# A third combined block a layer in a four-branch decoder trunk: 256 features of two branches side by side

## Chip, cores and metric

The kernel runs on one core of a Trainium2 chip. The metric is the device time of one execution in microseconds (us), the median of several runs; a profiled execution gives the trace.

## What is computed

Two layers on x of 512 tokens by 1024 features, in float32. In each, h = rmsnorm(x) is projected to the inputs of four token mixers, which give four branch outputs o of 256 features each, to four gates and to 4 x 1024 merge logits. What the change touches is the end of a layer:

```python
for i, o in enumerate((o_nsa, o_pool, o_conv, o_fox)):
    branch = (o * jax.nn.silu(gates[:, :, i])) @ w_branch[i]
    term = jax.nn.sigmoid(merge[:, :, i]) * branch
    acc = term if acc is None else acc + term
return x + acc @ w_out
```

`merge` is h times 1024 x 4096 weights, `w_branch[i]` is 256 x 1024 and `w_out` 1024 x 1024.

## The kernel before, in words

**Products.** TensorE (PE) takes a rounded 32-bit format, so every operand is split into a high and a low part, and a product is three matmuls (high-high, low-high, high-low). `split` makes the parts: ACT copies to the high part (L72), VectorE (DVE) subtracts for the low one (L73).

**Weights.** `Stream` (L93) brings the 80 weight tiles of a layer (128 x 1024, 512 KB) from `w_all`, in a fixed order, on the queue of SyncE (SP), into three buffers "wr". A tile's buffer is free again when DVE has made its low part. From `more` (L137) on, the merge weights may also go into four other places: the buffer of the rope tables and the three thirds of "V", the attention values, which come free with the last product of probabilities and V (L698). Two weights that are to be added are either added by DVE (L928) or by an accumulating load on the POOL queue (L125).

**A layer.** Dense projections (`dense`, L288: 24 matmuls of 128 x 512 at L303, evacuated by DVE at L324), then 12 attention units (scores L652, softmax on DVE and ACT L655 to L667, transposes L676, products with V L698) with `filler` dense projections between them, among them the first merge logits (`LOGITS`; `AHEAD` = 2 tiles are taken ahead). Then the end of the layer, in three parts:
- the dense part: features 0 to 511 of the merge, 16 logit tiles in feature-major form. For each m of four (L1224), `branches(m)` (L821, 24 matmuls at L832; evacuated at L837 and L841) and four `dense` of `LOGITS`. Between the matmuls of these goes `combine_h` (L850), 20 side steps and four more: it loads x tiles again ("ptc", two buffers, SP, L860), scales them on ACT (L867), sums them on DVE (L877 to L885) and splits the sums, four each for the products P7, P6, P3 and P5.
- `merge` (L955): features 512 to 1023 in two combined blocks, each of two branches, with tokens and inputs in halves. Seven products P1, P2, P7, P6, P5, P3, P4 (L988; 168 matmuls of 512 columns) give what eight would (192). P7 and P6 need the sums of x. Then 48 branch matmuls (L1026), tanh on ACT, sums on DVE. `prepare` (L909) and `merge_ahead` add and split the weights one or two products ahead.
- transposes to feature-major form, the output projection, and the residual; in layer 1 in two halves of the tokens, followed by the last norm. `add_square` and `sum_squares` (L230 to L260) make the norm's sum of squares.

**What sets the order.** The program is recorded in the order of the code and then reordered: a scheduler puts each engine's instructions into one fixed sequence, and each engine (and each engine's DMA queue) takes its own strictly in that order, waiting where a semaphore asks for it.

Of the kernel before, what the change touches and what calls it, by code (L numbers as in the profile page):

```python
# [20 lines left out]
NTILE = 80  # L21
MERGE0 = 52
FILL = 7
ACT_NORM = ()
HID = (9, 11, 13, 15)
GATES = [(0, 0), (2, 0), (0, 1), (2, 1), (1, 0), (3, 0), (1, 1), (3, 1)]
LOGITS = [(m, i) for m in range(4) for i in range(4)]
AHEAD = 2
# [16 lines left out]
def trunk_kernel(ctx: ExitStack, tc: tile.TileContext, xT, w_all, par_all, const, gains, rope, outT):  # L45
# [11 lines left out]
    def sb(shape, tag, bufs, dt=F32):  # L57
        return work.tile(shape, dt, tag=tag, name=tag, bufs=bufs)
# [34 lines left out]
    class Stream:  # L93
        def __init__(self):
            self.order, self.added = [], set()
            for l in range(L):
                self.order += [(l, i) for i in range(MERGE0)]
                for b in range(2):
# [12 lines left out]
            self.raw, self.parts = {}, {}  # L111
# [42 lines left out]
        def load(self, slot="wr"):  # L154
            i = self.loaded
            self.loaded += 1
            c = self.cols(i)
            self.slots.pop(next(n for n, x in enumerate(self.slots) if x is slot))
            if slot == "wr":
                t = sb([128, 1024], "wr", 3)  # L160
            elif slot == "rope":
                t = sb([128, 2, T], "rope", 1).rearrange("p a b -> p (a b)")
            else:
                t = slot
            l, j = self.order[i]
            if i == 0:
                for n in range(2):
                    nc.scalar.dma_start(t[:, n * 512:n * 512 + 512], w_all[l, j, :, n * 512:n * 512 + 512])
            else:
                nc.sync.dma_start(t[:, :c], w_all[l, j, :, :c])  # L170
            self.raw[i] = t, slot
# [65 lines left out]

    def add_square(src, m, bias=0.0, sq=None):
        n = src.shape[-1]
        sq = (temp() if sq is None else sq)[:, :n]  # L240
        ACT.activation(sq, src, AF.Square, bias=bias)
        if m in (0, 7):
            state["sq"] = sq
        else:
# [4 lines left out]
            else:  # L249
                DVE.tensor_tensor(state["sq"], state["sq"], sq, ALU.add)  # L250
            if m == 6:
                sum_squares(n, True, False)

    def stats(n=T, keep=False):
        sum_squares(n, False, True)
        p = state["ssq"]
# [652 lines left out]
    def prepare():  # L909
# [10 lines left out]

        for blk in range(2):
            t2 = [None, None]
# [32 lines left out]
    def merge(l, side, ah, al, lead):  # L955
# [6 lines left out]
        def tanh(dst, src, tok):  # L962
            ACT.activation(dst, src, AF.Tanh, scale=rth[:, tok:tok + 1])

        acc = [None] * 4
        for bp in range(2):
            X = Y = W = None
            sig = {}
            s1, u2, u4 = [None] * 2, [None] * 2, [None] * 2
            for name in PRODUCTS:  # L970
                if name == "P1":
# [8 lines left out]
                for h in range(2):  # L980
                    wh, wl = take_ready()
                    for tt in range(2):
# [8 lines left out]
                        if h == 0 and tt == 0:  # L991
                            merge_ahead(2)
                    merge_ahead(2)
                for tt in range(2):
                    if name in ("P1", "P6", "P5"):
                        t = sb([128, T], "p", 5) if name == "P5" and bp == 0 else temp()
                        ACT.activation(t, X[tt], AF.Copy)
                        {"P1": s1, "P6": u2, "P5": u4}[name][tt] = t
# [8 lines left out]
                    elif name == "P3":  # L1007
                        t = temp() if bp else sb([128, T], "p", 5)
                        tanh(t, X[tt], 4 + tt)
# [7 lines left out]
            for j, toks in ((1, (2, 3, 0, 1)), (0, (0, 1, 2, 3))):  # L1017
                wh, wl = take_ready()
                for tok in toks:
                    p = psum(*next(banks))  # L1020
                    n = 0
                    for kt in range(2):
                        yh, yl = state["y"][2 * bp + j, kt]
                        c, d = slice(tok * 128, tok * 128 + 128), slice(kt * 512, kt * 512 + 512)
                        for x, w in ((yh, wh), (yl, wh), (yh, wl)):
                            PE.matmul(p, x[:, c], w[:, d], start=(n == 0), stop=(n == 5))  # L1026
                            n += 1
                    sg = sig[j, tok]
# [15 lines left out]
        for f in range(4):  # L1044
            pt = psum("pt", 2)
            for tok in range(4):
                PE.transpose(pt[:, tok * 128:tok * 128 + 128], acc[tok][:, f * 128:f * 128 + 128], ident)
            h, lo = sb([128, T], "y", 16, F32R), sb([128, T], "y", 16, F32R)
            split(h, lo, pt, scale=0.5)
            ah.append(h)  # L1050
            al.append(lo)


    nc.gpsimd.dma_start(ng, gains)
    xr = []
# [16 lines left out]
    idle = psum("s", 2)  # L1072
    for n in range(16):
        PE.matmul(idle[:, 128:T], tri_ones[:, 128:256], tri_ones[:, 128:T], start=n == 0, stop=n == 15)

# [18 lines left out]
    for l in range(L):  # L1094
# [140 lines left out]
        if l + 1 < L:  # L1235
# [13 lines left out]
        else:  # L1249
            xn = []  # L1250

            def ev_last(m, c):
                def g(acc):
# [3 lines left out]
                    DVE.tensor_tensor(x, acc[:, :c.stop - c.start], x, ALU.add)  # L1257
                    add_square(x, m)
                    if m == 1:
# [29 lines left out]
    for half in range(2):  # L1289
# [3 lines left out]
        drain()  # L1293
        _, rb = stats(T // 2, keep=True)
        x = xn[KT - 1][:, c]
# [56 lines left out]
def _layout(np, a):  # L1352
# [8 lines left out]
    for l in range(L):  # L1361
# [22 lines left out]
        logit = [feat(run(3472 + 1024 * i + 128 * m)) for m, i in LOGITS]  # L1384
        for m in range(4):
            tiles += logit[4 * m + (AHEAD if m else 0):4 * m + 4 + AHEAD]
            tiles.append(a["w_branch"][l].reshape(8, 128, 1024)[:, :, m * 128:m * 128 + 128]
                         .transpose(1, 0, 2).reshape(128, 1024))
        for bp in range(2):
            for kh in range(2):  # L1390
# [44 lines left out]
```

## Time and profile before

| | before |
|---|---|
| median of 3 runs | 954.16 us (953.74 to 955.42) |
| profiled execution | 953.55 us |
| span of its trace | 951.0 us |
| PE busy | 936.2 us, 98% |
| DVE busy | 714.0 us, 75% |
| ACT busy | 520.0 us, 55% |
| DMA | 124.73 MB, mean 131 GB/s |

The span is the time between the trace's first and last event; the execution's own time has 2.6 us around it. Busy time is the sum of what an engine worked; the chain is the work and the waits that lead to the end, followed backwards. A group's mean is of its instructions' own durations, and PE's matmuls overlap, so a stream's pace is taken from the chain, not from the mean.

### The profile page before, as it was taken

To read this page: it belongs to the slowest core of one execution; us is meant where nothing else is said; L and a number is where in the kernel's file an instruction comes from. 1 tells how busy PE (TensorE), PEld (TensorE's weight loads), DVE (VectorE), ACT (ScalarE), POOL (GpSimd) and SP (SyncE) were. 2 spreads that over 40 slices of the span, in tenths; PEclk is the share of its full clock that TensorE was granted. 3 is DMA by queue.
4 is the path that set the end of the run, shared out by engine and by line. 5 is a ranking of instruction groups with operands and counts; after the bars stand their busy time and mean duration, and the time that the engine had idled before them with its cause. 6 is when DMAs were issued, how large, how long until landed. Compare 5 with 4: busy or idle time off the path is not lost.

```text
span 951.0 us, 12852 instructions
## 1 busy us (share of the span) xinstructions
PE 936.2 (98%) x4696; PEld 795.4 (84%) x4696; DVE 714.0 (75%) x1392; ACT 520.0 (55%) x906; POOL 31.1 (3%) x45
## 2 busy tenths in 40 slices
PE   9999999999999999999999999999999999999996
PEld 7988888888878888887889888888888788888796
DVE  6694689986787977776668548999677878686765
ACT  7295475575545554544426636656665455546273
POOL 0000000000000000000100000000000000010002
PEclk9999999999999999999999999999999999999998
DMA  7253222222236667643515421221322557686353
GB/s 268 80 175 113 74 83 68 78 89 89 67 122 173 171 207 213 177 155 134 189 63 170 135 89 67 89 67 45 111 67 79 177 159 201 200 210 194 112 168 121
DMA packets 39614, 124.73 MB, mean 131 GB/s; under 512 B 4464, under 2 KB 6528, under 8 KB 39552
## 3 DMA queue, kind: packets, MB, share of 16 engines
q1 hardware_dynamic: 35712, 112.38, 36.0%
q0 software_dynamic: 2976, 10.50, 5.5%
q10 hardware_dynamic: 864, 1.05, 0.3%
q8 instruction: 36, 0.59, 0.3%
q14 instruction: 26, 0.21, 0.1%
HBM read 119.72 MB, written 4.19 MB: 130 GB/s over the span
## 4 chain that ended last, share of the span: by engine, by line
PE 95%; DVE 2%; ACT 1%; DMA 1%; issue 1%; POOL 0%; DVEq 0%; SPq 0%; ACTq 0%; POOLq 0%
PE ps_d L303 56%; PE ps_d L988 9%; PE ps_s L988 5%; PE ps_o L698 3%; PE ps_pt L676 3%; PE ps_pt L988 2%; PE ps_pt L1026 2%; PE ps_s L554 2%; PE ps_pt L554 2%; PE ps_s L832 2%; PE ps_s L653 2%; PE ps_s L652 1%; PE ps_pt L832 1%; PE ps_o L1026 1%; PE ps_d L1026 1%; PE ps_o L415 1%
## 5 line engine op out<-in xcount | busy, mean ns | idle before, releaser
L303 PE MATMUL ps_d<-xh,wh 128*128 128x512 f32 x632 | 248.9, 394 | 1.9 <-ACT wh L72 1.9
L303 PE MATMUL ps_d<-xl,wh 128*128 128x512 f32 x632 | 248.6, 394 | 0.5 <-DVE xl L76 0.5
L72 ACT ACTIVATE wh<-wr 128x1024 fp32r<-128x1024 f32 (+2 forms) x134 | 139.0, 1038 | 153.9 <-PE ps_d L303 70.1
L73 DVE TENSOR_TENSOR wl<-wr,wh 128x1024 fp32r<-128x1024 f32 (+2 forms) x134 | 160.3, 1199 | 52.5 <-ACT wh L72 50.8
L303 PE MATMUL ps_d<-xh,wl 128*128 128x512 f32 x632 | 174.0, 392 | 0.0
L303 PEld LDWEIGHTS ps_d<-xh,wh 128*128 128x128 f32 x632 | 118.9, 188 | 25.7 <-ACT wh L72 3.0
L303 PEld LDWEIGHTS ps_d<-xl,wh 128*128 128x128 f32 x632 | 118.8, 188 | 24.0 <-DVE xl L76 1.5
L303 PEld LDWEIGHTS ps_d<-xh,wl 128*128 128x128 f32 x632 | 117.5, 188 | 23.1
L657 ACT ACTIVATE p<-p,nm 128x128 f32<-128x128 f32 (+1 forms) x96 | 53.3, 556 | 35.1 <-DVE nm L655 34.8
L324 DVE TENSOR_TENSOR t<-ps_d,rstd 128x512 f32<-128x512 f32 x74 | 50.7, 685 | 26.7 <-PE ps_d L303 26.3
L655 DVE CUSTOM_DVE_ANT_0 p<-ps_s,cst 128x128 f32<-128x128 f32 (+1 forms) x96 | 45.6, 484 | 13.0 <-PE ps_s L653 6.8
L72 ACT ACTIVATE ptx<-ps_pt 128x384 fp32r<-128x384 f32 (+1 forms) x72 | 36.9, 521 | 23.1 <-PE ps_o L698 14.3
L698 PE MATMUL ps_o<-ptx,V 128*128 128x256 f32 (+1 forms) x288 | 48.8, 282 | 0.6 <-DVE ptx L73 0.6
L698 PEld LDWEIGHTS ps_o<-ptx,V 128*128 128x128 f32 x288 | 42.4, 190 | 3.6 <-DVE ptx L73 0.8
L73 DVE TENSOR_TENSOR ptx<-ps_pt,ptx 128x384 fp32r<-128x384 f32 (+1 forms) x72 | 42.0, 592 | 2.1 <-ACT ptx L72 2.0
L676 PE MATMUL ps_pt<-cst,p 128*128 128x128 f32 x240 | 40.1, 276 | 0.0
L303 PE MATMUL ps_d<-y,wh 128*128 128x256 f32 (+1 forms) x176 | 38.0, 336 | 0.9 <-ACT y L75 0.9
L303 PE MATMUL ps_d<-st,wh 128*128 128x256 f32 (+1 forms) x176 | 33.5, 332 | 0.0
L73 DVE TENSOR_TENSOR wl<-V,wh 128x1024 fp32r<-128x1024 f32 x18 | 22.0, 1222 | 13.1 <-ACT wh L72 13.1
L303 PEld LDWEIGHTS ps_d<-y,wh 128*128 128x128 f32 x176 | 27.9, 190 | 4.2 <-ACT y L75 1.4
L72 ACT ACTIVATE wh<-V 128x1024 fp32r<-128x1024 f32 x18 | 19.1, 1062 | 21.9 <-PE ps_s L832 6.5
L676 PEld LDWEIGHTS ps_pt<-cst,p 128*128 128x128 f32 x240 | 28.1, 140 | 3.3
(343 smaller groups left out, 1736.4 us busy)
## 6 DMA issues: line engine op xcount, KB each, us to landing
wr<-in_w_all_dram SPq DMA_DIRECT2D x143, 512.0 KB, 3.3
V<-in_w_all_dram SPq DMA_DIRECT2D x26, 512.0 KB, 3.5
rope<-in_w_all_dram SPq DMA_DIRECT2D x12, 512.0 KB, 4.6
t<-in_xT_dram SPq DMA_DIRECT2D x16, 256.0 KB, 4.6
V<-in_w_all_dram POOLq DMA_DIRECT2D x8, 512.0 KB, 8.2
wr<-in_w_all_dram SPq DMA_DIRECT2D x8, 400.0 KB, 3.1
wr<-in_w_all_dram POOLq DMA_DIRECT2D x6, 512.0 KB, 6.8
ptc<-in_xT_dram SPq DMA_DIRECT2D x8, 256.0 KB, 3.1
```

Of the source, the lines that this page charges most:

```text
L72: ACT.activation(hi, src, AF.Copy)
L73: DVE.tensor_tensor(lo, src, f32(hi), ALU.subtract)
L303: PE.matmul(acc[:, :width], w, r[k][:, tok], start=(n == 0), stop=(n == 23))
L324: DVE.tensor_tensor(t, acc, state["rb"], ALU.mult)
L554: PE.matmul(accs[tt][:, 0:400], x[:, tt * 128:tt * 128 + 128], w, start=(k == 0 and a == 0), stop=(kp == 3 and kk == 1 and a == 2))
L655: DVE.tensor_tensor_reduce(out=P[:, :n], in0=s[:, :n], in1=bias, scale=1.0, scalar=3e38, op0=ALU.add, op1=ALU.min, accum_out=nm)
L657: ACT.activation(P[:, :n], P[:, :n], AF.Exp, bias=nm, scale=-1.0, accum_out=sm)
L676: PE.transpose(p[:, c:c + 128], self.P[qt][:, kb * 128:kb * 128 + 128], ident)
L698: PE.matmul(dst, V[:, kb, self.vset, :], part[:, src], start=(self.fresh and self.cmp is None and b == 0 and kb == 0 and j == 0), stop=(se ...
L832: PE.matmul(p, w[:, c], r, start=(n == 0), stop=(n == 5))
L988: PE.matmul(bank[tt], x, w[:, d], start=(opens and k == 0 and n == 0), stop=(name in ("P2", "P3", "P4") and k == 3 and n == 2), skip_group ...
L1026: PE.matmul(p, x[:, c], w[:, d], start=(n == 0), stop=(n == 5))
```

## The change

The dense part keeps features 0 to 255 (`LOGITS` of 2 x 4 tiles, two rounds of m). `merge` has a block more, the first: block 0 takes features 256 to 511 of all four branches, two branches side by side as the 512 columns of a weight tile (branches 0 and 1 take the place of a block's first branch, 2 and 3 of its second). Its logits come from the same seven products; its branch products are 96 matmuls of 256 columns instead of 48 of 512, and DVE adds the two halves of each sum. Its transposes (two features) go into block 1, after P1 there, the others stay at the end. The number of weight tiles is the same; a layer has four accumulating loads more. The side steps go after every fourth matmul of a dense projection, of which two are left for them; what remains of the 20 runs in one go after the two rounds.

Three small edits go with it: the gains are loaded on the ACT queue between two halves of the first weight tile, instead of on POOL's; 14 idle matmuls run at the start instead of 16; the sum of squares is made in one pass on PE after DVE has added all tiles, except in the last half of the last projection, which keeps two.

```diff
-MERGE0 = 52
+MERGE0 = 42
-LOGITS = [(m, i) for m in range(4) for i in range(4)]
+LOGITS = [(m, i) for m in range(2) for i in range(4)]
...
                     nc.scalar.dma_start(t[:, n * 512:n * 512 + 512], w_all[l, j, :, n * 512:n * 512 + 512])
+                    if n == 0:
+                        nc.scalar.dma_start(ng, gains)
...
-        if m in (0, 7):
+        if m == 0 or (m == 7 and two):
             state["sq"] = sq
...
-            if m == 6:
+            if m == 6 and two:
                 sum_squares(n, True, False)
...
-        for blk in range(2):
+        for blk in range(3):
             t2 = [None, None]
...
+        def by_rows(acc, n):
+
+            for f in range(n):
+                pt = psum("pt", 2)
+                for tok in range(4):
+                    PE.transpose(pt[:, tok * 128:tok * 128 + 128], acc[tok][:, f * 128:f * 128 + 128], ident)
+                tag = ("st", 20) if len(ah) < 4 else ("y", 16)
+                h, lo = sb([128, T], *tag, F32R), sb([128, T], *tag, F32R)
+                split(h, lo, pt, scale=0.5)
...
-        for bp in range(2):
+
+        for blk in range(3):
...
+                if blk == 1 and name == "P1":
+                    by_rows(first, 2)
...
-                    for kt in range(2):
-                        yh, yl = state["y"][2 * bp + j, kt]
-                        c, d = slice(tok * 128, tok * 128 + 128), slice(kt * 512, kt * 512 + 512)
-                        for x, w in ((yh, wh), (yl, wh), (yh, wl)):
-                            PE.matmul(p, x[:, c], w[:, d], start=(n == 0), stop=(n == 5))
-                            n += 1
+                    c = slice(tok * 128, tok * 128 + 128)
+                    two, width = (2, 256) if blk == 0 else (1, 512)
+                    for e in range(two):
+                        for kt in range(2):
+                            yh, yl = state["y"][(2 * j + e, kt) if blk == 0 else (2 * blk - 2 + j, kt)]
+                            d = slice(kt * 512 + e * width, kt * 512 + e * width + width)
+                            for x, w in ((yh, wh), (yl, wh), (yh, wl)):
+                                PE.matmul(p[:, e * width:e * width + width], x[:, c], w[:, d], start=(n == 0),
+                                          stop=(n == 6 * two - 1), skip_group_check=True)
+                                n += 1
...
+            if blk == 0:
+                for tok in range(4):
+                    DVE.tensor_tensor(acc[tok][:, 0:256], acc[tok][:, 0:256], acc[tok][:, 256:512], ALU.add)
+                first, acc = acc, [None] * 4
...
-        for m in range(4):
+        for m in range(2):
             if m == 1:
                 ws.more()
             a, b = branches(m)
+            ah.append(a)
+            al.append(b)
             for mi in LOGITS[4 * m + 4 + AHEAD:4 * m + 8 + AHEAD]:
                 for n, _ in enumerate(dense(rhs, ev_merge(*mi))):
-                    if n % 12 == 11 and steps:
+                    if n % 4 == 3 and steps:
                         next(side)
                         steps -= 1
-            ah.append(a)
-            al.append(b)
+        for _ in range(steps):
+            next(side)
```

The scheduler's order of the instructions on PE at the end of attention in layer 0. Before (L303 are the dense projections, L832 the branch products; 14 rows of L303 alike stand ahead of these):

```order
L303 MATMUL ps_d<-xh,wh 128x512
L303 MATMUL ps_d<-xl,wh 128x512
L698 MATMUL ps_o<-ptx,V 128x256
L303 MATMUL ps_d<-xh,wl 128x512 x7
L303 MATMUL ps_d<-xh,wh 128x512
L303 MATMUL ps_d<-xl,wh 128x512
L303 MATMUL ps_d<-xh,wl 128x512
L698 MATMUL ps_o<-ptx,V 128x256
L698 MATMUL ps_o<-ptx,V 128x128 x2
L676 MATMUL ps_pt<-cst,p 128x128 x7
L652 MATMUL ps_s<-st 128x512
L653 MATMUL ps_s<-st 128x512
```

In the changed kernel (L700 is the old L698, L678 the old L676, L654 and L655 the old L652 and L653, L834 the old L832; no L305, the old L303, stands behind its first row):

```order
L305 MATMUL ps_d<-xh,wl 128x512
L654 MATMUL ps_s<-st 128x256
L655 MATMUL ps_s<-st 128x256
L654 MATMUL ps_s<-st 128x384
L655 MATMUL ps_s<-st 128x384
L700 MATMUL ps_o<-ptx,V 128x256 x2
L700 MATMUL ps_o<-ptx,V 128x128 x2
L678 MATMUL ps_pt<-cst,p 128x128 x4
L654 MATMUL ps_s<-st 128x512
L655 MATMUL ps_s<-st 128x512
L678 MATMUL ps_pt<-cst,p 128x128 x3
L834 MATMUL ps_s<-y,wh 128x512 x2
```

The 48 dense matmuls of this place, two projections, are gone, and the branch products follow the attention pieces directly.

SP's queue in the same stretch, where "ptc" are the x tiles of the side steps (L862, the old L860), and "wr", "V" and "rope" weight tiles. Before:

```order
L860 DMA ptc<-in_xT_dram 128x512
L170 DMA wr<-in_w_all_dram 128x1024
L170 DMA V<-in_w_all_dram 128x1024 x4
L170 DMA wr<-in_w_all_dram 128x1024 x2
L860 DMA ptc<-in_xT_dram 128x512
L170 DMA wr<-in_w_all_dram 128x1024
L860 DMA ptc<-in_xT_dram 128x512
L170 DMA wr<-in_w_all_dram 128x1024
L860 DMA ptc<-in_xT_dram 128x512
L170 DMA wr<-in_w_all_dram 128x1024
```

In the changed kernel:

```order
L862 DMA ptc<-in_xT_dram 128x512
L172 DMA V<-in_w_all_dram 128x1024 x3
L172 DMA wr<-in_w_all_dram 128x1024 x3
L862 DMA ptc<-in_xT_dram 128x512
L172 DMA wr<-in_w_all_dram 128x1024
L172 DMA rope<-in_w_all_dram 128x1024
L172 DMA V<-in_w_all_dram 128x1024
L862 DMA ptc<-in_xT_dram 128x512
L172 DMA V<-in_w_all_dram 128x1024
L862 DMA ptc<-in_xT_dram 128x512
L172 DMA wr<-in_w_all_dram 128x1024
L862 DMA ptc<-in_xT_dram 128x512 x2
```

Each queue has the same loads of x. In the changed kernel the weight tiles between them are all of the first combined block, in V and "rope" too, and each waits until DVE has split or added what lay in its buffer.

DVE in the changed kernel from the split of P7's first tile on ("ptx" from "V", L73), with the splits and adds (L930, the old L928) of the weights of P2, P7 and P6 and the sums of the side steps (L880 to L887, the old L878 to L885):

```order
L73 TENSOR_TENSOR ptx<-V,ptx 128x1024
L76 SCALAR_TENSOR_TENSOR st<-t,st 128x512
L73 TENSOR_TENSOR st<-p,st 128x256 x3
L73 TENSOR_TENSOR st<-ptc,st 128x256
L76 SCALAR_TENSOR_TENSOR st<-t,st 128x512
L930 TENSOR_TENSOR V<-V,wr 128x1024
L73 TENSOR_TENSOR wl<-rope,wh 128x1024
L73 TENSOR_TENSOR wl<-V,wh 128x1024
L880 TENSOR_TENSOR p<-ptc 128x256
L1018 TENSOR_TENSOR t<-ps_pt,t 128x512
L930 TENSOR_TENSOR V<-V 128x1024
L883 SCALAR_TENSOR_TENSOR p<-p,ptc 128x256
```

Before, the side steps' sums stand between evacuations of dense projections, and all of them ahead of the first addition of two weights (L928).

## Rows read from the trace of the kernel before

**Rows 1.** The page: span, busy time of each engine, chain by engine.
```profile
span 951.0 us, 12852 instructions
...
PE 936.2 (98%) x4696; PEld 795.4 (84%) x4696; DVE 714.0 (75%) x1392; ACT 520.0 (55%) x906; POOL 31.1 (3%) x45
...
PE 95%; DVE 2%; ACT 1%; DMA 1%; issue 1%; POOL 0%; DVEq 0%; SPq 0%; ACTq 0%; POOLq 0%
```

**Rows 2.** Waits of PE, 250 to 335 (layer 0), then 715 to 800 (layer 1).
```profile
PE ps_s L832 <- DVE y L711: 0.9, 1, 0.9
PE ps_d L303 <- ACT wh L72: 0.8, 1, 0.8
...
PE ps_d L303 <- ACT wh L72: 1.1, 1, 1.1
PE ps_s L832 <- DVE y L711: 0.2, 1, 0.2
```

**Rows 3.** Busy time by stretch of layer 0; columns as in the first line.
```profile
core 0: us, PE busy (x) PEld busy (x) DVE busy (x) ACT busy (x) POOL busy (x), PEclk, DMA share, GB/s
255.00:272.00 17.00, 17.00 (x91) 14.51 (x90) 12.51 (x28) 8.05 (x17) 0.00 (x0) 1.00 0.19 63
272.00:285.00 13.00, 12.06 (x62) 9.22 (x60) 11.96 (x20) 6.34 (x11) 0.00 (x0) 1.00 0.54 182
285.00:312.00 27.00, 26.19 (x116) 21.69 (x116) 21.26 (x34) 13.72 (x23) 0.92 (x1) 1.00 0.64 181
312.00:330.00 18.00, 18.00 (x81) 14.89 (x80) 16.36 (x29) 9.42 (x17) 1.73 (x2) 1.00 0.67 155
330.00:384.00 54.00, 54.00 (x240) 44.57 (x239) 40.45 (x44) 27.86 (x35) 3.42 (x4) 1.00 0.69 199
384.00:433.00 49.00, 49.00 (x219) 40.45 (x218) 35.18 (x41) 22.79 (x28) 0.86 (x1) 1.00 0.55 163
```

**Rows 4.** The chain, 255 to 285: start us, us, what.
```profile
255.97 3.20 PE ps_d L303 x14
...
259.28 2.29 PE ps_d L303 x10
...
261.86 0.79 PE ps_pt L676 x7
...
264.49 4.31 PE ps_d L303 x19
...
269.38 0.70 PE ps_d L303 x3
...
277.93 0.30 PE ps_o L698 x3
...
278.25 0.33 SPq L170
...
278.63 4.53 DMA V<-in_w_all_dram
```

**Rows 5.** The chain, 320 to 345, then 890 to 945.
```profile
329.64 2.72 PE ps_d L988 x12
...
340.52 4.53 PE ps_s L988 x20
...
926.80 0.34 PE ps_o L235 x4
...
931.04 10.57 PE ps_d L303 x88
...
944.19 0.72 PE ps_o L263 x4
```

**Rows 6.** The chain, 0 to 12.
```profile
1.27 4.71 DMA ng<-in_gains_dram
...
6.00 0.73 ACT xh L75
```

**Rows 7.** Timeline of DVE, 253 to 262.
```profile
256.61 0.68 DVE L324 TENSOR_TENSOR t<-ps_d,rstd 128x512 f32<-128x512 f32 x1
257.21 0.55 DVE L73 TENSOR_TENSOR ptx<-ps_pt,ptx 128x384 fp32r<-128x384 f32 x1
...
260.01 0.42 DVE L667 TENSOR_SCALAR p<-p,sm 128x384 f32<-128x384 f32 x1
```

**Rows 8.** DMA issues, 255 to 335: median us to landing in the last column.
```profile
ptc<-in_xT_dram SPq DMA_DIRECT2D x6, 256.0 KB, 3.1
...
V<-in_w_all_dram POOLq DMA_DIRECT2D x1, 512.0 KB, 8.5
```

**Rows 9.** ACT by line and form, 250 to 335.
```profile
L867 ACT ACTIVATE ptc<-ptc,ng 128x512 f32<-128x512 f32 x6 | 4.3, 722 | 5.8 <-DMA ptc<-in_xT_dram 5.8
```

**Rows 10.** DVE by line and form, 250 to 335.
```profile
L73 DVE TENSOR_TENSOR wl<-wr,wh 128x1024 fp32r<-128x1024 f32 x11 | 13.4, 1223 | 4.4 <-ACT wh L72 3.1 <-ACT ptx L72 1.2
L841 DVE TENSOR_TENSOR t<-t 128x512 f32<-128x512 f32 x12 | 8.1, 686 | 0.1
...
L73 DVE TENSOR_TENSOR st<-p,st 128x256 fp32r<-128x256 f32 x8 | 3.2, 421 | 0.0
```

**Rows 11.** Busy time and granted clock (PEclk) at the end.
```profile
943.00:945.00 2.00, 0.87 (x6) 0.59 (x5) 0.16 (x1) 0.05 (x2) 0.69 (x1) 1.00 0.00 0
945.00:947.00 2.00, 0.00 (x0) 0.00 (x0) 1.59 (x5) 0.38 (x1) 1.41 (x2) 0.80 0.14 51
947.00:949.00 2.00, 0.00 (x0) 0.00 (x0) 0.49 (x2) 0.00 (x0) 0.00 (x0) 0.50 1.06 369
```

More of the change, by code (lines that the diff above doesn't have):

```diff
@@ L97, in __init__ @@
                 self.order += [(l, i) for i in range(MERGE0)]
-                for b in range(2):
+                for b in range(3):
                     o = MERGE0 + 10 * b
@@ L236, in sum_squares, with add_square @@
                       start=(first and tt == 0), stop=(last and tt == n // 128 - 1))
-    def add_square(src, m, bias=0.0, sq=None):
+    def add_square(src, m, bias=0.0, sq=None, two=False):
         n = src.shape[-1]
@@ L250, in add_square, with stats @@
                 DVE.tensor_tensor(state["sq"], state["sq"], sq, ALU.add)
-            if m == 6:
+            if m == 6 and two:
                 sum_squares(n, True, False)
-    def stats(n=T, keep=False):
-        sum_squares(n, False, True)
+    def stats(n=T, keep=False, two=False):
+        sum_squares(n, not two, True)
         p = state["ssq"]
@@ L963, in tanh @@
             ACT.activation(dst, src, AF.Tanh, scale=rth[:, tok:tok + 1])
+        def by_rows(acc, n):
[6 more added lines that the diff above has]
+                split(h, lo, pt, scale=0.5)
+                ah.append(h)
+                al.append(lo)
         acc = [None] * 4
-        for bp in range(2):
+        for blk in range(3):
             X = Y = W = None
@@ L969, in merge @@
             s1, u2, u4 = [None] * 2, [None] * 2, [None] * 2
+            stay = blk < 2
             for name in PRODUCTS:
@@ L993, in merge @@
                     merge_ahead(2)
+                if blk == 1 and name == "P1":
+                    by_rows(first, 2)
                 for tt in range(2):
                     if name in ("P1", "P6", "P5"):
-                        t = sb([128, T], "p", 5) if name == "P5" and bp == 0 else temp()
+                        t = sb([128, T], "p", 5) if name == "P5" and stay else temp()
                         ACT.activation(t, X[tt], AF.Copy)
@@ L1007, in merge @@
                     elif name == "P3":
-                        t = temp() if bp else sb([128, T], "p", 5)
+                        t = sb([128, T], "p", 5) if stay else temp()
                         tanh(t, X[tt], 4 + tt)
@@ L1042, in merge @@
                 next(g)
[L1044 to L1054, printed above, removed]
+        by_rows(acc, 4)
     xr = []
@@ L1072, in trunk_kernel @@
     idle = psum("s", 2)
-    for n in range(16):
-        PE.matmul(idle[:, 128:T], tri_ones[:, 128:256], tri_ones[:, 128:T], start=n == 0, stop=n == 15)
+    for n in range(14):
+        PE.matmul(idle[:, 128:T], tri_ones[:, 128:256], tri_ones[:, 128:T], start=n == 0, stop=n == 13)
     def x_parts(k, src, g):
@@ L1257, in g @@
                     DVE.tensor_tensor(x, acc[:, :c.stop - c.start], x, ALU.add)
-                    add_square(x, m)
+                    add_square(x, m, two=c.start > 0)
                     if m == 1:
@@ L1293, in trunk_kernel @@
         drain()
-        _, rb = stats(T // 2, keep=True)
+        _, rb = stats(T // 2, keep=True, two=half == 1)
         x = xn[KT - 1][:, c]
@@ L1384, in _layout @@
         logit = [feat(run(3472 + 1024 * i + 128 * m)) for m, i in LOGITS]
-        for m in range(4):
+        for m in range(2):
             tiles += logit[4 * m + (AHEAD if m else 0):4 * m + 4 + AHEAD]
@@ L1388, in _layout @@
                          .transpose(1, 0, 2).reshape(128, 1024))
+        cat = lambda parts: np.concatenate(parts, axis=1)
+        for kh in range(2):
+            for j in range(2):
+                tiles += pairs(cat([w[512 * kh:512 * kh + 512, 3728 + 1024 * i:3984 + 1024 * i]
+                                    for i in (2 * j, 2 * j + 1)]))
+        for j in range(2):
+            tiles += pairs(cat([a["w_branch"][l, i][:, 256:512] for i in (2 * j, 2 * j + 1)]))
         for bp in range(2):
```

## Prediction

> **What bounds the kernel now.** I read the page first: TensorE (PE) is busy 936.2 of 951.0 us, VectorE (DVE) 75% of the span, and the chain that ended last is PE for 95% [rows 1]. The profiled execution took 953.55 us, 0.61 below the median of 954.16; the sum below is made against 953.55. An average of 98% says that columns taken from PE come off the time. Whether they do is decided where the columns are taken, so I read the waits of PE next: around the end of attention in layer 0 two, 1.7 us together, and in the same place of layer 1 two, 1.3 us together [rows 2]. That is little, but the table by stage says how it is achieved: DVE is busy 12.51 of 17 us, then 11.96 of 13, 21.26 of 27 and 16.36 of 18, and 40.45 of 54 in the first combined block [rows 3]. From the end of attention to the end of the dense part DVE has next to no slack of its own (85% over 272 to 330), and PE is full because dense projections are free to run whenever an attention or a merge step is late. The chain shows it: 48 matmuls of dense work, 10.9 us, stand between the attention pieces from 255.97 to 271 [rows 4].
>
> **What leaves PE.** A 512-column matmul takes 0.2265 us in a stream (20 in 4.53), a 256-column one 0.120 (88 in 10.57), a transpose 0.113 (7 in 0.79), and four records of the sum of squares 0.34 [rows 5, 4]. Counted from the order, both layers together: 144 matmuls of 512 columns go, 32.6 us; 192 of 256 columns come (the branch products of the new block, of half the width and twice the number), 23.0 us; 16 transposes come, 1.8 us; 20 records of the sum of squares go, 1.7 us. PE's own work falls by 9.5 us. That DVE adds the squares instead (0.69 us each, one a layer) lies beside projections, which hide it; without that cover it would be under 2 us. Two idle matmuls fewer before the first projection cost and gain nothing: PE waits there for data.
>
> **The start.** The first projection is released by the gains: their load took 4.71 us from the POOL queue, and the first split of x runs at 6.00 [rows 6]. It moves to the ACT queue, between two halves of the first weight tile. I take 0.5 us off; bounds 0 (x and the weights land at about the same time) and 0.8.
>
> **What the lost cover costs.** Until 255.8 us the order on PE is the same. Behind that point the 48 dense matmuls are gone: the dense part has 8 logit tiles instead of 16, and all are used up. I walked the new order of layer 0 with durations of these rows; layer 1 has the same order.
> (1) To the last product of attention's probabilities with V (277.93 before [rows 4]). What is left for PE is some 5.4 us of attention and 24 branch matmuls, 5.4 us: 10.9. DVE has the last softmax, its splits, the head's output, and beside them the side steps' sums and the branch products' evacuations: from the last normalisation, which ended at 260.4 [rows 7], 22 instructions of 11.0 us that overlap by 0.08 each, 9.3 us, then the last split, transposed tile and product, 2 us. The end comes at 271.8, 16 us for 10.9 us of PE work: 5.1 us idle.
> (2) The second branch group, the first half of P2 and P1 follow. P1's weights go into "wh" buffers that the last branch matmuls free, and on DVE stand behind five half-width evacuations and sums. A further 3.3 us idle.
> (3) The first base tiles of P7 are put into V's thirds, free only at 271.8. The load from there took 4.53 us behind 0.38 of issue [rows 4], and POOL's accumulating load on it 8.5 [rows 8]: 285 to 286.5. ACT and DVE take their work in order, and the split of this tile stands ahead of the split of P2's second half in both. 2.5 us idle. In before the same sort of load is issued at 278 and on with 50 us to spare before the block begins at 329.6 [rows 5].
> (4) P7 and P6 need the sums of x from the side steps. Before, the steps ran between dense projections and were done before the block began. Now 8 of 20 run in one go, and their loads stand on SP behind weight tiles that wait for DVE. The second tile of step 1 goes out at about 286; the next pair waits for DVE's split at about 302 (behind 286.5 come 20 DVE instructions in order, 16.7 us, 14.9 with the overlap), the last pair for the one after. Each link is 3.1 us of load [rows 8], 0.72 of scaling on ACT [rows 9] and 2 to 3 on DVE and ACT. The last matmul of P6 ends at about 316.5; 11.7 us idle.
> PE's work from 255.8 to there is 38.1 us (48 branch matmuls 10.9, 96 of P1, P2, P7 and P6 21.8, attention 5.4), so without stalls it would end at 293.9: 22.6 us idle. **Bounds.** Below: DVE alone, if no load and no buffer came late. Its 79 instructions from the last softmax to the last operand of P6 are 13 of 1.22 us, 26 of 0.69, 32 of 0.42 and 8 small ones, 50.4 us [rows 10]; since one starts about 0.08 before the one ahead has ended (256.61 to 257.21 for one of 0.68 [rows 7]), 44.2. From 260.4 that gives 304.6 and, with the last six matmuls, 306: 12 us idle. Above: the walk, 22.6. I take 20, nearer to the walk, since ACT, DVE and SP are all strictly in order in it and I found nothing that would let P7 overtake. From P5 on, the new block and the two old ones are like those of before, which ran 54.00 of 54 us busy with DVE at 75% [rows 3], and I add nothing; DVE's 20 more full-width operations lie mostly in that block's split and are in the sum above.
>
> The sum: −9.5 for PE's work, −3.0 for the old waits, which stand where the new ones do, −0.5 at the start, +2 × 20: +27, so 980.5 against 953.55, and 981 by the median. The bounds give −13 + 2 × 12 = +11 and −13 + 2 × 22.6 = +32.
>
> The Trainium skill, "Perfetto Trace Analysis", Optimization Strategy, says that a kernel whose most-contended engine changes over time may gain from interleaving the regimes; by it, taking dense work (PE's regime) away from attention and the side steps (DVE's) speaks against the change, as the rows do. The same page, Identifying the Most-Contended Engine, says to improve the engine of the highest occupancy first: by that alone PE's 9.5 us would come off.
>
> **Rivals.** (A) Faster: PE stays the bound everywhere and only its work counts, 953.55 − 13 = 941. For it: 98% busy PE and 95% of the chain [rows 1], and combined blocks that ran without a gap. Against it: DVE's 44.2 us against some 33 of PE behind 260.4. It decides for faster if the idle time is below 5.5 us a layer, half of what the sum gains without stalls (11 to 13), so DVE's operations would have to wait for one another less, or be fewer in that stretch, than I counted: the side steps mostly done under attention.
> (B) Slower, but only by DVE's work: loads come in time, 12 us a layer, 966.
> (C) Slower, and the clock with it. Here PE's granted clock is 1.00 in every stretch but the end, where it is 0.80 in 945 to 947 and 0.50, the 1.2 GHz level, in 947 to 949, with no matmul since 944.9 [rows 5, 11]. If gaps of some us between P7 and P6 do that, their 48 matmuls run at half the pace, 10.9 us more a layer, of which about half shows because they wait anyway: 992; all of it, 1002. The Trainium skill, "TensorE: Matmul & The Clock Gate", Part 1, says that an idle TensorE falls to half clock and rises again with sustained work; the end of this trace agrees, no gap inside it does.
> (D) The order does not do as the diff says, for instance P1 to P7 running with the old count: excluded, the listing has 144 fewer wide matmuls.
>
> **Chances.** The forecast 0.52; B 0.17; C 0.13; A 0.15; a place between A and no change or just past it 0.03. Two thousandths of the time, 1.9 us, is about what a measurement can tell from no change: faster by more than that 0.15, within it 0.03, slower 0.82. The range leaves out A and the upper end of C: 958 to 999.
>
> **What would show it.** In the profile of the changed kernel, PE's busy time should be about 927 (936.2 − 9.5), more if the clock falls. The waits of PE between 255 and 317 should sum to about 20 us, ended by DVE's softmax and splits, by the split of P7's first tile (behind POOL's load), and by side steps' operands at P7 and P6; the same in layer 1. DVE should be busy over 80% from 260 to 305. The two later blocks should each take the 49 us of before without waits. Wrong it would be if PE's waits in that stretch were under 6 us, which would mean that the side steps or P7's tiles come earlier than by my walk, or if the blocks after it waited for weight tiles instead.

## Result and profile after

The changed kernel takes **996.45 us** (993.58 to 998.02, 4 runs) against 953.95 for the kernel before on the same chip: a ratio of 1.0441, 95% interval 1.0425 to 1.0457, 42.5 us slower. It lies inside the range of 958 to 999, 15.5 us above the 981 that were named.

The page of the changed kernel, span, busy time and the chain by engine:

```profile
span 994.3 us, 13054 instructions
...
PE 949.5 (95%) x4738; PEld 797.0 (80%) x4738; DVE 735.0 (74%) x1415; ACT 540.4 (54%) x930; POOL 36.9 (4%) x52
...
PE 86%; DVE 5%; DMA 5%; ACT 2%; issue 1%; POOL 0%; SPq 0%; DVEq 0%; ACTq 0%; POOLq 0%
```

Against [rows 1] the span is 43.3 us longer. PE's share of the chain fell from 95% to 86%, and DVE, the DMAs and ACT took what it lost. PE's busy time rose by 13.3 us although its work fell; the granted clock, below, is the larger part of the reason. PE's idle time (span less busy time) rose by 30.0 us, from 14.8 to 44.8.

The waits of PE in layer 0, 250 to 340 (us in total, times, longest):

```profile
PE ps_s L1004 <- ACT st L72: 3.5, 1, 3.5
PE ps_d L1004 <- ACT wh L72: 3.1, 2, 2.6
PE ps_pt L1004 <- ACT wh L72: 2.1, 1, 2.1
PE ps_d L1004 <- DVE wl L73: 1.9, 2, 1.0
PE ps_o L700 <- DVE ptx L73: 1.7, 1, 1.7
PE ps_d L1004 <- ACT st L72: 1.5, 1, 1.5
PE ps_pt L834 <- DVE t L839: 0.6, 1, 0.6
PE ps_s L1004 <- ACT wh L72: 0.4, 1, 0.4
```

These are 14.8 us where [rows 2] had 1.7. Four of the eight lines, 7.5 us, are for weights of the first combined block (wh, wl), two (ACT st), 5.0 us, for the operands of P7 and P6 that the side steps make. The list of layer 1 (735 to 830) is much the same, 15.4 us in all.

Busy time by stretch, columns as in the first line:

```profile
core 0: us, PE busy (x) PEld busy (x) DVE busy (x) ACT busy (x) POOL busy (x), PEclk, DMA share, GB/s
255.00:272.00 17.00, 15.12 (x78) 12.26 (x77) 15.28 (x35) 9.74 (x20) 0.00 (x0) 0.90 0.15 47
272.00:285.00 13.00, 10.93 (x46) 8.06 (x45) 11.56 (x17) 2.64 (x3) 1.94 (x2) 1.00 0.94 250
285.00:300.00 15.00, 9.85 (x40) 6.88 (x39) 11.11 (x17) 9.83 (x16) 1.72 (x2) 0.99 0.83 231
300.00:312.00 12.00, 8.65 (x23) 5.43 (x22) 8.99 (x16) 5.75 (x11) 0.00 (x0) 0.72 0.59 192
312.00:320.00 8.00, 5.45 (x13) 3.93 (x13) 4.51 (x10) 4.72 (x9) 0.00 (x0) 0.59 0.26 89
320.00:330.00 10.00, 10.00 (x45) 8.32 (x45) 4.97 (x5) 6.25 (x9) 0.00 (x0) 0.99 0.56 169
405.00:455.00 50.00, 50.00 (x224) 41.29 (x223) 35.46 (x41) 22.75 (x28) 0.87 (x1) 1.00 0.57 171
...
254.90:334.70 79.80, 64.79 (x260) 48.87 (x259) 58.93 (x99) 42.65 (x70) 3.66 (x4) 0.89 0.56 162
743.50:821.10 77.60, 61.93 (x249) 46.83 (x248) 56.55 (x89) 41.57 (x66) 3.53 (x4) 0.91 0.56 167
```

Set beside [rows 3], PE was 17.00 of 17 us busy from 255 to 272 and is 15.12 now; from 285 to 320 it is busy 23.95 of 35. And PEclk, 1.00 in all of [rows 3], is 0.90, then 0.72 and 0.59 from 300 to 320. The two levels are 1.2 and 2.4 GHz, so a mean of 0.59 is mostly the lower one. The third block (405 to 455) runs as before, 50.00 of 50. The last two lines are two longer stretches, one in each layer, that are used below.

The chain from 252 to 340, some of its longest pieces (start us, us, what):

```profile
259.23 2.56 PE ps_s L834 x6
...
266.14 2.78 DMA ptc<-in_xT_dram
...
277.87 7.76 DMA V<-in_w_all_dram
...
290.00 5.23 DMA ptc<-in_xT_dram
...
302.16 3.37 PE ps_d L1004 x7
...
308.74 3.65 DMA ptc<-in_xT_dram
...
314.55 2.93 PE ps_s L1004 x6
317.48 11.01 PE ps_d L1004 x42
```

Here are the loads that the prediction named, on the path: the x tiles (ptc) at 266, 290 and 308.74, and the accumulating load into V of 7.76 us that lands at 285.63. The matmul pieces show the clock: six at 259.23 took 0.427 us each, seven at 302.16 0.481, six at 314.55 0.488, 42 behind that 0.262, where a stream has 0.2265 [rows 5]. Above that pace they are 1.2, 1.8, 1.6 and 1.5 us: 6.1 us of slow matmuls on the chain of one layer, all but a little of it the lower clock (at half the pace a matmul would take 0.453).

A mark for the comparisons below is the first branch product of the new block. Its matmuls' first and last start in layer 0, changed kernel (count, ns, first to last start in us):

```profile
L1047 PE MATMUL ps_pt<-ptx,y x36: 278/283/389, 334.7 to 449.7; 128*128 128x256 f32 x24, 128*128 128x512 f32 x12
```

If nothing waited, the 259 matmuls between the last common dense matmul (its end at 254.9) and this mark would take 53.4 us at the paces of [rows 5, 4]: 48 branch and 160 products of 512 columns, 47.1, and 6.3 of attention (28 products with V, 17 transposes, six score matmuls of 2304 columns together). That would put the mark at 308.3. It stands at 334.7: **26.4 us lost in layer 0**. PE was idle for 15.0 of them (64.79 of 79.80 us busy), and busy for 11.4 longer than those 53.4. Counted in the same way from 743.5, layer 1 lost 25.7: 51.9 us of work, and the mark at 821.1; 15.7 idle, 10.0 of longer busy time. So about two fifths of the loss are not waits but matmuls that took longer. The clock can be at most 8.8 of the 11.4 in layer 0 (a mean of 0.89 over 79.80 us is 17.6 us at the lower level); what the rest is was not taken apart.

### The profile page after: what moved, and what is told of

The parts are those of the page before. It is cut to its first block, busy times and chain, and to the rows that moved or that the text cites. A ratio compares the mean times of both kernels' runs of the same rounds, so it can differ in the third digit from the quotient of the medians.

```text
span 994.3 us, 13054 instructions
## 1 busy us (share of the span) xinstructions
PE 949.5 (95%) x4738; PEld 797.0 (80%) x4738; DVE 735.0 (74%) x1415; ACT 540.4 (54%) x930; POOL 36.9 (4%) x52
## 4 chain that ended last, share of the span: by engine, by line
PE 86%; DVE 5%; DMA 5%; ACT 2%; issue 1%; POOL 0%; SPq 0%; DVEq 0%; ACTq 0%; POOLq 0%
PE ps_d L305 44%; PE ps_d L1004 12%; PE ps_s L1004 6%; PE ps_pt L1047 3%; PE ps_o L700 3%; PE ps_pt L678 2%; PE ps_pt L1004 2%; PE ps_s L556 2%; PE ps_pt L556 2%; PE ps_d L1047 2%; PE ps_o L1047 2%; DMA V<-in_w_all_dram 2%; PE ps_s L655 1%; DVE ptx L73 1%; PE ps_s L654 1%; DMA ptc<-in_xT_dram 1%
## 5 line engine op out<-in xcount | busy, mean ns | idle before, releaser
L73 DVE TENSOR_TENSOR wl<-wr,wh 128x1024 fp32r<-128x1024 f32 (+2 forms) x130 | 155.8, 1199 | 62.8 <-ACT wh L72 61.3
L305 PE MATMUL ps_d<-xl,wh 128*128 128x512 f32 x504 | 198.7, 395 | 0.6 <-DVE xl L76 0.6
L305 PE MATMUL ps_d<-xh,wh 128*128 128x512 f32 x504 | 198.4, 395 | 0.5 <-ACT wh L72 0.3
L305 PE MATMUL ps_d<-xh,wl 128*128 128x512 f32 x504 | 140.2, 393 | 0.0
L305 PEld LDWEIGHTS ps_d<-xl,wh 128*128 128x128 f32 x504 | 94.8, 188 | 19.5 <-DVE xl L76 1.8
L305 PEld LDWEIGHTS ps_d<-xh,wh 128*128 128x128 f32 x504 | 94.7, 188 | 19.1 <-ACT wh L72 0.9
L305 PEld LDWEIGHTS ps_d<-xh,wl 128*128 128x128 f32 x504 | 93.5, 188 | 18.3
L659 ACT ACTIVATE p<-p,nm 128x128 f32<-128x128 f32 (+1 forms) x96 | 53.3, 556 | 30.7 <-DVE nm L657 30.4
L326 DVE TENSOR_TENSOR t<-ps_d,rstd 128x512 f32<-128x512 f32 x58 | 39.8, 686 | 24.1 <-PE ps_d L305 23.9
L700 PE MATMUL ps_o<-ptx,V 128*128 128x256 f32 (+1 forms) x288 | 50.0, 287 | 2.8 <-DVE ptx L73 2.3
L1004 PE MATMUL ps_d<-wh,st 128*128 128x512 f32 x128 | 43.5, 427 | 8.0 <-ACT wh L72 5.3
L700 PEld LDWEIGHTS ps_o<-ptx,V 128*128 128x128 f32 x288 | 43.0, 193 | 7.1 <-DVE ptx L73 3.3
L73 DVE TENSOR_TENSOR ptx<-ps_pt,ptx 128x384 fp32r<-128x384 f32 (+1 forms) x72 | 41.9, 594 | 1.6 <-ACT ptx L72 1.6
L678 PE MATMUL ps_pt<-cst,p 128*128 128x128 f32 x240 | 41.0, 278 | 0.0
L1004 PEld LDWEIGHTS ps_d<-wh,st 128*128 128x128 f32 x128 | 25.8, 205 | 16.6 <-ACT wh L72 7.1
L305 PE MATMUL ps_d<-y,wh 128*128 128x256 f32 (+1 forms) x176 | 37.9, 335 | 0.9 <-ACT y L75 0.9
L73 DVE TENSOR_TENSOR wl<-V,wh 128x1024 fp32r<-128x1024 f32 x24 | 29.2, 1224 | 10.9 <-ACT wh L72 10.6
L305 PE MATMUL ps_d<-st,wh 128*128 128x256 f32 (+1 forms) x176 | 33.6, 332 | 0.0
```

What stands on the lines that cost most here:

```text
L73: DVE.tensor_tensor(lo, src, f32(hi), ALU.subtract)
L305: PE.matmul(acc[:, :width], w, r[k][:, tok], start=(n == 0), stop=(n == 23))
L326: DVE.tensor_tensor(t, acc, state["rb"], ALU.mult)
L659: ACT.activation(P[:, :n], P[:, :n], AF.Exp, bias=nm, scale=-1.0, accum_out=sm)
L678: PE.transpose(p[:, c:c + 128], self.P[qt][:, kb * 128:kb * 128 + 128], ident)
L700: PE.matmul(dst, V[:, kb, self.vset, :], part[:, src], start=(self.fresh and self.cmp is None and b == 0 and kb == 0 and j == 0), stop=(se ...
```

## Experiments

Each number is a single execution unless an interval stands with it. The kernel before took 952.50 to 953.65 beside them.

| kernel | us | mark in layer 0 | mark in layer 1 |
|---|---|---|---|
| changed kernel | 996.45 | 334.7 | 821.1 |
| fillers at 5 a step | 994.51 | 334.0 | 819.5 |
| side steps early | 972.33 | 322.2 | 797.2 |
| both | 967.05 | 318.0 | 791.5 |
| no side steps | 961.38 | 318.1 | 786.3 |
| no side steps, fillers at 5 | 960.11 | 316.5 | 784.9 |
| the same, no accumulating load on P7 | 961.39 | 317.2 | 786.2 |

The theory at the start was that of the prediction: the time goes into waits behind attention, where dense work no longer covers late operands. Its rivals were the new block itself (256-column products, more accumulating loads) and DVE's amount of work.

**1. The small edits alone**, on the kernel before (gains on ACT's queue, 14 idle matmuls, one pass of the sum of squares).

> The kernel before with the three small edits alone (gains on the ACT queue, 14 idle matmuls, sum of squares in one pass). The theory (the lost time is waits behind attention) expects these edits to be innocent: 20 records of the sum of squares at 0.085 us leave PE, up to 0.5 us more or less at the start, so 951 to 954 against 953.95. If they cost part of the 42 us, it should come out above 956.

953.15 us, ratio 0.9993, interval 0.9982 to 1.0003: no difference. The start gained nothing, which its chain explains (start us, us, what):

```profile
2.12 6.25 DMA wr<-in_w_all_dram
...
8.39 1.07 ACT wh L72
...
9.51 2.65 PE ps_d L305 x10
```

The first dense matmul starts at 9.51, against 9.49 in the kernel before. The gains gate it no longer, but the load of a weight tile of 6.25 us does, in their place.

**2. No side steps.**

```diff
-        h, lo = state["S"][name][k]
-        return h[:, c], lo[:, c]
+        return xh[k][:, c], xl[k][:, c]
...
-        side = combine_h(l)
-        steps = 20
+        side, steps = iter(()), 0
```

> The changed kernel without the side steps: P7, P6, P3 and P5 read x itself instead of the sums, so the sums are left out. Theory: the last third of the lost time is operands of P7 and P6 that come late, 11.7 us idle a layer by the walk, and the low clock that follows from it; without them 966 to 975. Rival 1, that the third block itself is dear (256-column products, more accumulating loads): within 4 us of 996.5. Rival 2, DVE alone bounds: 32 operations of 0.42 a layer go from DVE, 25 us in both layers, so about 971 too, but then with DVE busy over 95% from 260 to 300.

961.38 us, below what was expected: 35 of the 42.5 us go with the side steps. The new block with its 256-column products and its loads is all there, so the rival that it is dear in itself falls. The rival that DVE alone bounds misses too: it wanted about 971 with DVE over 95% busy, and DVE is busy 31.46 of 40 us from 260 to 300. The edit takes away the steps' loads and their work on ACT and DVE together; whether their lateness or their amount costs the time is for the next experiment.

**3. The side steps early**, same work.

```diff
         side = itertools.chain(decay(l), cmp_attention())
+        sums, steps = combine_h(l), 20
...
             for _ in range(FILL):
                 next(fill, None)
+            if s >= 37 and steps:
+                next(sums)
+                steps -= 1
...
-        side = combine_h(l)
-        steps = 20
+        side = sums
```

> The changed kernel, same work; the 20 side steps are recorded one a step in the last third of attention instead of behind it, so their loads and sums stand ahead of the block's weight tiles on SP and DVE. Theory (the wait is for loads and sums that stand late in order): 968 to 980, P7 and P6 without waits for st, attention some us longer. Rival 2 (DVE's amount of work is the bound): no gain, 990 to 1000, as DVE does the same work in the same stretch. Rival 1 (the block itself): within 4 us of 996.5.

972.33 us, as the theory had it, and not the 990 to 1000 of the rival "DVE's amount of work": 24 us back with no work taken away (PE, DVE and ACT have the same counts as in the changed kernel):

```profile
PE 939.8 (97%) x4738; PEld 791.6 (82%) x4738; DVE 732.1 (75%) x1415; ACT 540.1 (56%) x930; POOL 36.9 (4%) x52
```

PE's busy time fell by 9.7 us, its idle time (30.7 of a span of 970.5) by 14.1: the gain is waits and slow matmuls together. From 300 to 320, where the clock had been 0.72 and 0.59, it is 1.00. The mark moved up by 12.5 us:

```profile
L1047 PE MATMUL ps_pt<-ptx,y x36: 277/284/390, 322.2 to 437.2; 128*128 128x256 f32 x24, 128*128 128x512 f32 x12
```

The waits of PE from 200 to 345, of which these are the three longest of nine, name no operand of the side steps (st) any more:

```profile
PE ps_o L700 <- ACT ptx L72: 1.4, 1, 1.4
PE ps_d L1004 <- DVE wl L73: 1.3, 2, 1.0
PE ps_pt L834 <- DVE t L839: 1.2, 1, 1.2
```

**4. Fillers at 5 a step** (`FILL = 5`), which leaves dense matmuls to stand beside the last attention units.

> The changed kernel, same work; filler matmuls go into attention at 5 a step instead of 7, so 41 dense matmuls that ran earlier now stand beside its last units. Theory: it gives back the 5.1 us idle a layer to the last product with V, at most 8 with the clock, none of the rest: 980 to 990. Rival 1: within 4 us of 996.5.

994.51 us: a miss. Attention's last product with V moved up, from a start at 271.0 to 268.1, but the mark only from 334.7 to 334.0: what was gained before 272 was waited away behind it, for weights and sums (the longest waits of PE from 250 to 340 are 3.8, 3.7 and 3.1 us, for wh, st and wh).

**5 and 6. Both together**, with the side steps from step 37 and from step 33.

> The side steps recorded early (as in the run before) and fillers at 5 a step together. Theory: with the sums out of the way (972.3 alone), the end of attention is next on the path, and dense work beside it pays: 960 to 968. Rival (POOL's load on P7's first tile, which waits for V and stands ahead of P2's split on ACT and DVE, sets the start of the block in any case): 970 to 973, the idle time moved from before 272 to behind it.

> As e5, with the side steps four steps of attention earlier (from step 33 instead of 37), so that DVE has done more of them before attention's last unit. Theory (DVE is full around the end of attention): 1 to 4 us below e5. Rival (V's buffer sets the start of P7): same as e5 within 2.

967.05 and 967.33 us. With the sums out of the way the fillers pay 5 us, near the upper end of what was expected; starting the sums earlier still adds nothing. The first is the fastest version that leaves nothing out, and 13.8 us slower than the kernel before. DVE is full in that one at the end of attention:

```profile
255.00:265.00 10.00, 8.34 (x43) 6.71 (x41) 9.54 (x22) 6.76 (x15) 0.00 (x0) 0.83 0.17 56
265.00:275.00 10.00, 9.01 (x48) 7.04 (x46) 9.87 (x19) 6.22 (x13) 0.46 (x1) 1.00 0.57 191
275.00:285.00 10.00, 8.04 (x33) 5.67 (x32) 9.41 (x16) 3.59 (x6) 1.52 (x2) 1.00 0.87 218
```

DVE's are 9.54, 9.87 and 9.41, 28.82 of 30 us. That made DVE's amount of work the next suspect, tried in 9 to 11. Experiment 6 speaks a little against it already: DVE was busy 26.98 of the same 30 us there, and the time was the same.

**7. Side steps early, no accumulating loads on P7's tiles.**

```diff
-                    nc.gpsimd.dma_start(t, w_all[l, j], accum_op=ALU.add)
+                    if j not in (MERGE0 + 2, MERGE0 + 3):
+                        nc.gpsimd.dma_start(t, w_all[l, j], accum_op=ALU.add)
```

> The changed kernel with the side steps early (972.3) and without the two accumulating loads a layer on P7's tiles of the first combined block; their second weights are left out of the sum. Theory (the split of P7's first tile waits for V, a load and POOL's accumulating load, and holds up P2's split behind it): the tile is ready 8 us earlier, P2 and P7 start up to 3 us earlier a layer, 965 to 970. If DVE's work alone sets that stretch: 971 to 973.

975.31 us: a miss, no gain over 972.33. The accumulating load is on the chain of the changed kernel and of experiment 5 (9.45 us there), and not on this one's from 240 to 330; but PE starts P7 no sooner, at 300.46 against 294.75 in experiment 3. In its place this chain has DVE's evacuations of the branch products, the low part of P1's weights, and 20 matmuls that take 7.41 us: the picture of experiment 12, below.

**8. More work for PE among P7 and P6**, to see whether the low clock or the operands set that stretch.

```diff
+                            if blk == 0 and name in ("P7", "P6"):
+                                for n in range(3):
+                                    PE.matmul(warm, a, wh[:, d], start=True, stop=True)
```

> The changed kernel with 48 added matmuls a layer among those of P7 and P6, each a repeat of one that has just run, into a bank that nobody reads: 10.9 us more work a layer at full clock. Theory (the arrival of operands sets the time, and the low clock costs part): between -8 and +5 us against 996.5, granted clock over 0.9 from 300 to 320. If the clock cost nothing and PE were the bound: +22. If only the arrival counted and the clock cost nothing: 0 to +6.

1006.77 us (1004.88 to 1010.61; ratio to the kernel before 1.0567, interval 1.0538 to 1.0596): 10.3 us above the changed kernel, outside both what the theory and what its rivals named. Of the 21.8 us of added work, half showed in the span (994.3 to 1004.9). The rest went two ways: PE's idle time fell by 5.2 us (44.8 to 39.6), and its busy time rose by only 15.8 (949.5 to 965.3), so that some 6 us came back from matmuls that ran faster or closer together. The clock rose less than was meant (285 to 320):

```profile
285.00:300.00 15.00, 12.37 (x47) 9.12 (x45) 9.84 (x15) 8.17 (x15) 1.72 (x2) 0.89 0.77 205
300.00:312.00 12.00, 8.67 (x27) 5.88 (x27) 8.31 (x16) 6.23 (x11) 0.00 (x0) 0.86 0.44 148
312.00:320.00 8.00, 6.05 (x20) 4.54 (x19) 3.22 (x8) 3.11 (x6) 0.00 (x0) 0.79 0.11 40
```

0.72 and 0.59 became 0.86 and 0.79, but 0.99 became 0.89. So this does not tell the clock's price from the waits'; both had a part.

**9. No side steps, fillers at 5**, and **10 and 11, the side steps' low parts and then two of their sums on GpSimd** instead of DVE.

```diff
-                split(h, lo, t)
+                ACT.activation(h, t, AF.Copy)
+                POOL.tensor_tensor(lo, t, f32(h), ALU.subtract)
```

> The changed kernel without the side steps (as in e2, the sums left out) and with fillers at 5 a step. Theory now: with the sums early DVE is full from 255 to 285 (28.9 of 30 us in e5), so its amount of work there is what is left on the path; with the sums out and dense work at the end of attention, 950 to 956 against 961.4 with fillers at 7. If V's buffer and POOL's load set the start of P7: 959 to 962.

> The changed kernel, same result: side steps early (from step 33), fillers at 5, and the 16 low parts of the sums a layer on GpSimd instead of DVE (6.7 us less for DVE a layer; GpSimd is idle there and took 0.92 us for a product of this size). Theory (DVE's amount of work is what is left): 3 to 6 us less a layer than 967, so 955 to 961. If buffers or loads are: 965 to 968. If GpSimd's work disturbs DVE's: above 968.

> As e10, and two of the four sums of a side step on GpSimd too (8 more operations of 0.42 us a layer off DVE). Theory: 1 to 3 us a layer below e10, 950 to 958. If the sums, now a chain over GpSimd, come late again at P7 and P6: above e10.

960.11 us, and 969.56 (ratio to the kernel before 1.0169, interval 1.0152 to 1.0186) and 971.67 (1.0202, interval 1.0183 to 1.0220): three misses for the theory, each in the range that its expectation gave to a rival. That alone does not show those rivals' reasons. Leaving the sums out altogether (9) took 6.9 us off experiment 5, where the expected 950 to 956 would have been 11 to 17, though DVE was then busy only 23.68 of the 30 us from 255 to 285; beside experiment 2 the fillers were worth 1.3 us, less than single executions can tell apart. Moving 6.7 us a layer from DVE to GpSimd (10) was 2 us slower than experiment 6, a small difference beside a single execution. It is no test of DVE in that stretch: DVE was busy 26.60 of the 30 us there, against 26.98 in experiment 6, and the chain runs over V's buffer again (an accumulating load of 8.77 us). GpSimd took 1.02 us for one of these, where DVE took 0.42 [rows 10]:

```profile
L877 POOL TENSOR_TENSOR st<-p,st 128x256 fp32r<-128x256 f32 x16 | 16.3, 1018 | 81.2 <-ACT st L876 81.0
```

So DVE's amount of work alone is not what is left either; that rests on 6 and 9. In experiment 9, too, the chain runs over V's buffer:

```profile
272.01 1.06 POOL V L125
...
274.71 8.13 DMA V<-in_w_all_dram
```

**12. No side steps, fillers at 5, no accumulating loads on P7**: both suspects of 7 and 9 out at once.

> As e9 (no side steps, fillers at 5), and without the accumulating loads on P7's tiles as in e7: both left out at once. Theory: after the late sums, two chains of the same length are left, DVE's work to about 287 and V's buffer with its two loads to about 285, so that taking either alone gained nothing (e7 and e9); without both, P2 and P7 run 4 to 8 us earlier a layer, 946 to 955 against 960.1. If neither is what holds it: 958 to 962.

961.39 us, within the 958 to 962 of "neither": the theory of two equal chains falls too. What its chain shows from 276 on is a third one:

```profile
276.62 0.49 DVE t L840
...
277.22 0.68 DVE t L840
...
279.56 0.69 DVE t L844
280.24 1.15 DVE wl L73
...
281.44 7.67 PE ps_d L1004 x20
```

The last branch products are evacuated by DVE (t), and only behind them come the low parts of P1's weights, whose buffers those products held. PE waits, and its clock falls:

```profile
275.00:280.00 5.00, 3.25 (x13) 2.01 (x12) 3.81 (x6) 3.28 (x4) 0.00 (x0) 1.00 0.11 47
280.00:285.00 5.00, 3.56 (x8) 2.81 (x9) 4.86 (x6) 1.08 (x3) 0.00 (x0) 0.57 0.50 157
285.00:290.00 5.00, 5.00 (x18) 3.99 (x17) 1.23 (x1) 2.58 (x4) 1.94 (x2) 0.75 0.96 256
```

Twenty matmuls then take 7.67 us, 3.1 more than at full clock, and what was taken out of V's chain is of no use. Some 10 us a layer are left (961 against 941 for PE's work alone) that no single removal gave back, and what sets them is not shown. Whether they can be had, by freeing "wh" earlier or by another place for P1's weights, was not tried.

## Why the prediction held, and where it was short

**What leaves PE** could not be seen directly, since PE's busy time holds the low clock: 949.5 us instead of "about 927". The counts bear it out: -144, +192, +16, -20 and two idle matmuls less make 42 more, and the page has 4738 against 4696. And the sum closes: 953.55, less the 9.5 and the 3.0 of old waits, and 26.4 and 25.7 more in the two layers, is 993.2; PE's idle time outside those two stretches, 14.1 us instead of 11.8, makes it 995.5, against 996.09 in the profiled execution.

**The start**: 0.5 us were taken off for the gains. Experiment 1 shows 0: a weight tile landed as late, the bound that the prediction named. In the changed kernel's own trace the first dense matmul starts at 9.99, 0.5 later than before, behind an x tile whose load took 5.95 us.

**The times of the lost cover** came out close, on the changed kernel's chain. Last product with V: 271.8 predicted, its last start at 271.0; but PE was idle for 1.88 us from 255 to 272, where 5.1 had been forecast, and slower matmuls made up the rest, so that this agreement is in part luck. Accumulating load landed: 285 to 286.5, and 285.63. Second tile of step 1: issued at about 286, and 290.00. Next pair: 302 predicted, 298.64 and 303.94; the last pair went out from 308.74 on. P6's last matmul: 316.5, and 319.9 (317.48 and six matmuls of the 42, at the lower clock). The loads of x on the chain took 2.78, 5.23 and 3.65 us where [rows 8] gave 3.1. PE's waits were to sum to about 20 us and were 14.8, most of them for operands that were named. DVE was to be over 80% busy from 260 to 305, and was for 37.51 of 45 us.

**The step that was short** is "2 x 20" in the sum, which measured 26.4 and 25.7, 12.1 us more together. What it lacked is the clock. It forecast waits alone; the idle time was less than it said, 15.0 us, and slow matmuls took the rest. Of the 26.4 us in layer 0, 6.1 are slow matmuls on the chain; without them 20.3 would be left if nothing else came to stand on the path, which no run tried. The clock was left to rival C at "about half" of 10.9 us a layer, 992, with a chance of 0.13. Forecast and rival C came together, and C had too small a chance. That the time stayed inside a range that left out "the upper end of C" is in part luck. Some 3 us more of the miss are the start and short waits elsewhere, for which the sum had -0.5 and nothing.

**The rule on regimes** that was weighed against the change (the Trainium skill, "Perfetto Trace Analysis", Optimization Strategy) held: with 10.9 us of dense work a layer gone from DVE's stage, some 26 us a layer were lost. The Trainium skill, "TensorE: Matmul & The Clock Gate", Part 1, says that an idle TensorE falls to half clock. The trace agrees in the direction, and shows a fall without a long stop: PE had been busy for 1.28 of 3 us, and from 258 to 261 the granted clock was 0.64:

```profile
250.00:255.00 5.00, 5.00 (x33) 4.44 (x32) 2.53 (x11) 2.76 (x7) 0.00 (x0) 1.00 0.23 92
255.00:258.00 3.00, 1.28 (x10) 1.01 (x9) 3.00 (x7) 1.28 (x3) 0.00 (x0) 1.00 0.26 60
258.00:261.00 3.00, 3.00 (x13) 2.47 (x12) 2.90 (x10) 2.54 (x7) 0.00 (x0) 0.64 0.30 115
```

**Rival A** (941, PE the bound everywhere) is refuted by the result. **Rival B** (DVE's work alone, with the loads in time: 966) is not what happened; with the sums early the kernel came near its number (972 and 967), but experiment 6 relieved DVE by 1.8 us without a gain, and experiment 9 took all the sums off it for less than was expected, so the number alone doesn't bear the reason out.

**The places** of the loss were less separable than the four numbered steps made them look. Step 4, the late sums, was priced at 11.7 us a layer, and moving them is worth 12.5 alone (the mark in experiment 3), which is shown. The nearness of the two is in part luck: the price was for waits, and only 7.2 us of the 12.5 are idle time (15.0 to 7.8 up to the mark), the rest faster matmuls. Step 1 was priced at 5.1 and is worth 0.7 alone, 4.2 behind experiment 3 (the mark from 322.2 to 318.0). Step 2, priced at 3.3, was not tried. Step 3 was priced at 2.5, and taking its accumulating loads away gained nothing (experiments 7 and 12). Idle time in one place of a strictly ordered chain is not what its removal brings.

## What to carry to other kernels

Work that is free to run at any time can be worth more than its own length where it stands beside a stage that another engine bounds; before taking it away, ask what will be late there, and move that first. Here moving the side steps gave back 24 of 42.5 us, and nothing that was tried brought the time below the kernel before. Here the waits also cost twice: among them the granted clock fell (0.72 and 0.59 from 300 to 320), and the matmuls between them took longer. When stalls stand in a row, price their sum by a walk through the new order; take one alone as worth anything between nothing and its full length.

## What was not expected

The granted clock fell towards the 1.2 GHz level without a long stop: in the changed kernel it was 0.64 from 258 to 261, and the only wait that the profile lists in 250 to 262 is one of 1.7 us. Adding 21.8 us of matmuls cost 10.3. And an accumulating load, 7.76 us long and on the chain of the changed kernel, could be taken out of two later versions without any gain.
